# First projection block in three rounds over the banks, and two gathered blocks ahead of the first expert product

## The chip, the cores and the metric

The kernel runs on one core of one Trainium2 chip. The metric is device time in microseconds (us). TensorE is PE in the profile, VectorE is DVE, ScalarE is ACT, GpSimd is POOL, and SP is the engine whose queue issues nearly all DMAs. "PEld" is TensorE's weight load, "PEclk" its granted clock as a share of 2.4 GHz.

## What is computed

One encoder layer on 512 tokens of width 1024, all in float32. Cut to what matters here:

```python
mod = silu(c) @ w_ada + b_ada                     # shifts, scales, gates
u = x * (1.0 + sc_a) + sh_a
proj = u @ w_in                                   # queries, keys, values of two kinds of attention
mix = concat(latent_attention(proj), differential_attention(proj)) @ w_out
x = layer_norm(ALPHA * x + g_a * mix)
u = x * (1.0 + sc_f) + sh_f
aff = softmax(u @ w_router)                       # 16 experts, each takes its 64 best tokens
for e in range(16):
    xs = u[top64(aff[:, e])]
    y = (silu(xs @ w_gate[e]) * (xs @ w_up[e])) @ w_down[e]
    out[top64] += y * gate
x = layer_norm(ALPHA * x + g_f * out)
```

The expert weights (16 experts, three matrices of 8 MB each) are about 400 MB of the 456 MB that the kernel moves.

## The kernel before

**Three stages of order.** The start (the main projections, lines 425 to 483) and everything from the last output products on (router, experts, end) are written under a manual schedule: there each engine gets its instructions in the order of the text. Between them lies the attention stage. Its instructions are ordered by a scheduler that lays the program out against simulated times, so the order there depends on when it thinks the start is over.

**The start.** Inputs and weights come in 8 blocks of 128 input rows. For block i, `stage1_load` issues on SP's queue two rows of the modulation weights, the transposed input `xt` and the weights `wd`; one DMA waits for the DMA eight places ahead of it. DVE's `mod_finish` (L217) makes the block's shift and scale, and ACT (L433) makes the modulated input twice: rounded (`u.hi`) and in full (`xt`). Every float32 product is made of three products of the rounded format: both operands are split into a rounded high part and the low rest. `w_hi` on ACT (L136) and `w_lo` on DVE (L419) split the weights, L435 (DVE) makes `u.lo`. `mm3` issues the three products of one output one behind the other:

```python
    def mm3(o, l, r, start, stop):
        mm(o, l[0], r[0], start, False)
        mm(o, l[0], r[1], False, False)
        mm(o, l[1], r[0], False, stop)
```

For each block PE runs `mm3` on PSUM banks BK0 to BK3 (first half of the weights' columns), in block 0 two small products for the relative-position bias, and then `mm3` on BK4 to BK7 (second half). All products go through the helper at line 121. The banks gather over all 8 blocks and are read at the end.

In block 0, DVE's order is: shift and scale, `u.lo`, `w_lo` of the first half, `w_lo` of the second half.

**Behind the blocks.** SP's queue also carries the weights `w_q` of seven further projections (L326), and one large copy inside device memory, `bias_d<-f_d` (L481), which spreads the bias table to 512 rows of 3.5 KB. The source `f_d` is written in block 1 (L469), once DVE has copied the two small products (L145). The further projections use BK3 and BK7 in turn. Before a projection can run, ACT makes the high part of its weights (L136) and DVE the low part (L236); before its bank is used again, ACT and DVE read the bank (for keys: L136, then L501). The softmax of the differential attention is L549 (scores, PE), L564 (DVE) and L568 (ACT).

**The expert products.** 24 pages of 1 MB hold expert weights. Experts go in pairs. `up` (L1366) multiplies for each of 8 input blocks k the gathered tokens `xs[k]` with two pages (one for each expert), 16 matmuls in all, and frees both pages; SP's queue then issues the next two loads. The tokens of a pair are gathered by `gather`: 8 small matmuls for each block k with a 0/1 matrix, then one instruction of DVE (L1284, even k) or ACT (L1282, odd k) that scales and shifts. For the first pair no earlier work is there to hide the gathering, so `in_gate(k)` runs in front of product k: blocks 0 to 2 in front of product 0, then one block in front of each product, the last (block 7) in front of product 5; in front of product 7 stand the matrices for scattering back.

Of the kernel before, what the change touches and what calls it, by code (L numbers as in the profile page):

```python
# [101 lines left out]
def encoder_layer(ctx: ExitStack, tc: tile.TileContext, xT, x, wadaT, cvec, colp, rowp, rows, cst, pos, posr,  # L102
# [312 lines left out]
    def w_hi(i, c):  # L415
        EP["hi"] = hi_of(ACT, wsp[i][1].hi[:, c], st1[i][4][:, c])

    def w_lo(i, c):
        DVE.tensor_tensor(wsp[i][1].lo[:, c], st1[i][4][:, c], ff(wsp[i][1].hi[:, c]), op=OP.subtract)  # L419


    for i in range(KB):
        mw, hx, xt, hw, wd = st1[i]
        if i == 0:
            mod_finish(mw)
        if i < 2:
            w_page(i)
        if i == 0:
            w_hi(0, HALVES[0])
        uh, pg = pages.get(4, F32R)  # L430
        u = HL(pg[:, :512], pg[:, 512:])
        for dst in (u.hi, xt):
            ACT.activation(dst, xt, AF.Identity, scale=modc[:, 8 + i:9 + i], bias=modc[:, i:i + 1])  # L433
        if i < 2:
            DVE.tensor_tensor(u.lo, xt, ff(u.hi), op=OP.subtract)  # L435
            for c in HALVES:
                if i or c.start:
                    w_hi(i, c)
                w_lo(i, c)
        else:  # L440
            for c in HALVES:
                w_lo(i, c)
            DVE.tensor_tensor(u.lo, xt, ff(u.hi), op=OP.subtract)
        whh, wh = wsp.pop(i)
        U.append(u)
        Uh.append(uh)
        XT.append(xt)
        XTh.append(hx)
        pages.put(hw)
        if i + 2 < KB:  # L450
            stage1_load(i + 2)
        if 1 <= i < KB - 1:
            w_page(i + 1)
            for c in HALVES:
                w_hi(i + 1, c)
            mod_finish(st1[i + 1][0])
        for n in range(4):
            mm3(BK[n], wh[:, n * P:(n + 1) * P], u[:, :], i == 0, i == KB - 1)
        if i == 0:
            for c in range(2):  # L460
                mm(BK[6 + c][0:4, :], rb, ohp[:32, c * 512:(c + 1) * 512], True, True)
            mod_finish(st1[1][0])
            for c in range(2):
                copy(DVE, ohp[32:36, c * 512:(c + 1) * 512], BK[6 + c][0:4, :])
        for t in range(4):
            mm3(BK[4 + t], u[:, t * P:(t + 1) * P], wh[:, 512:1024], i == 0, i == KB - 1)
        pages.put(whh)
        if i == 1:
            SP.dma_start(f_d, ohp[32:36, :])  # L469
        if i == 2:  # L470
            bias_steps()
        if i == 4:
            bias_table()
        if i == 5:
            q_load(0)
            SP.dma_start(rowb[:, :R_W], bcast(rowp, R_W))
            SP.dma_start(subc, bass.AP(tensor=rowp.tensor, offset=rowp.offset + R_SUB, ap=[[1, P], [1, 1]]))
            SP.dma_start(csb, bass.AP(tensor=cst.tensor, offset=cst.offset, ap=[[C_W, P], [1, C_OH]]))
            RL = rope_load()
            q_load(1)  # L480
            SP.dma_start(bass.AP(tensor=bias_d.tensor, offset=bias_d.offset, ap=[[P * 1024, 4], [1024, P], [1, 896]]),  # L481
                         bass.AP(tensor=f_d.tensor, offset=f_d.offset + 127, ap=[[1024, 4], [-1, P], [1, 896]]))
# [1022 lines left out]
    for pr in range(NP):  # L1505
        G, U = HALF[pr % 2], HALF[1 - pr % 2]

        def in_gate(k, pr=pr, U=U):
            if pr == 0:
                gather(0, U[2:], (k + 2) * (k > 0), min(k + 3, KB))  # L1510
                if k == KB - 1:
                    scat_mats(0, *U[2:])
                return
            k0 = 3 if pr == 1 else 1
            if k0 <= k <= k0 + 3:
                for hf in range(2):
                    scatter(pr - 1, k - k0, hf, U[hf])
            elif k == k0 + 4:
                scat_mats(pr, *U[2:])
            elif k == 6 and pr == NP - 1:  # L1520
                spread(EP["l2"], U[2:], (1.0, 1.0))

        def in_up(c, G=G, U=U):
            hidden(c, U)
            if c:
                hidden_t(c - 1, G)

        def in_down(b, pr=pr, G=G):
            if b == 0:
                hidden_t(3, G)  # L1530
            if pr == NP - 1:
                if b >= 2:
                    for t in (2 * b - 4, 2 * b - 3):
                        mm(LB[t], ident, acc[t][:, 512:], True, False)
                return
            if b == 0:
                onehots(pr + 1)
            if 2 <= b <= 5:
                gather(pr + 1, G[:2], 2 * b - 4, 2 * b - 2)

        up(pr, "g", G, in_gate)
        gates(G)
        up(pr, "u", U, lambda k: None, in_up)
        down(pr, G[2:], in_down)
        if pr < NP - 1:
            for c in range(2):
                gated(c, G[2:])
        else:
            down_last()
# [78 lines left out]
```

## Time and profile before

| | |
|---|---|
| Median of 3 runs | 1246.4 us (1245.75 to 1248.85) |
| The profiled execution | 1248.78 us |
| Its span, first to last instruction | 1247.0 us |
| PE, DVE, ACT busy | 94%, 30%, 18% of the span |
| Mean granted TensorE clock | 0.989 |
| DMA | 456.03 MB, mean 366 GB/s |

Start to about 62 us, attention to about 290 us, choice of tokens to 307.6 us, experts to 1228 us, last normalisation to the end. Times in the rows are us from the span's start. In a timeline, a row begins with the start and the length of a run of equal instructions; what stands in brackets is the idle time of that engine before it and what ended it. PE's ends are modelled, so a busy PE can hide short waits.

### The profile page before, as it was taken

What the parts mean: (1) busy time and instruction counts of PE and PEld (TensorE: products, weight loads), DVE (VectorE), ACT (ScalarE), POOL (GpSimd) and SP (SyncE); (2) the same over time, 40 slices, a digit from 0 to 9 for tenths busy, and PEclk for the clock granted to TensorE, in tenths of its full rate; (3) what the DMA queues carried; (4) which work ended last, traced back from release to release, by engine and by line L of the source; (5) the groups of instructions that cost most, each with busy time, mean ns of one, the idle gap of its engine ahead of it and who ended that gap; (6) DMA issues with size and microseconds to landing.
All of it is one profiled execution on the core that took longest, in us unless ns stands there. A gap on an engine that the chain in (4) does not pass through costs nothing.

```text
span 1247.0 us, 14037 instructions
## 1 busy us (share of the span) xinstructions
PE 1166.6 (94%) x5657; PEld 553.3 (44%) x5657; DVE 373.9 (30%) x827; ACT 230.6 (18%) x473; POOL 34.0 (3%) x31
## 2 busy tenths in 40 slices
PE   8999999998999999999998899789979997999896
PEld 4877677765434333433432243234323432443232
DVE  6869989866001111111020102011101110111016
ACT  3556785433001000000000000000000000001001
POOL 0000000000000500000000000000000000000003
PEclk8999999998999999999999999999999999999999
DMA  8882516578999999999999999999999999999993
GB/s 339 307 294 74 200 62 212 195 323 342 370 420 421 420 421 421 421 421 421 420 422 420 422 421 421 422 421 421 422 421 422 421 422 420 420 422 420 422 397 144
DMA packets 76359, 456.03 MB, mean 366 GB/s; under 512 B 8284, under 2 KB 8668, under 8 KB 28162
## 3 DMA queue, kind: packets, MB, share of 16 engines
q1 hardware_dynamic: 76002, 455.02, 89.8%
q8 instruction: 44, 0.72, 0.2%
q14 instruction: 23, 0.19, 0.0%
q10 hardware_dynamic: 290, 0.10, 0.0%
HBM read 452.98 MB, written 3.95 MB: 366 GB/s over the span
## 4 chain that ended last, share of the span: by engine, by line
DMA 37%; PE 37%; DVE 1%; issue 0%; POOL 0%; ACT 0%; POOLq 0%; SPq 0%; DVEq 0%; ACTq 0%
PE bk L121 22%; DMA pg<-in_w_up_dram 18%; PE bk L1366 15%; DMA pg<-in_w_gate_dram 10%; DMA pg<-in_w_down_dram 10%; PE bk L1397 0%; DVE small L1240 0%; DVE ohg L1242 0%; POOL pg L1495 0%; DVE lst L1477 0%; PE bk L1290 0%; POOLq L1624 0%; PE bk L1315 0%; DVE mv L1478 0%; DVE pg L1434 0%
## 5 line engine op out<-in xcount | busy, mean ns | idle before, releaser
L1366 PE MATMUL bk<-pg,xs 128*64 128x512 f32 x2048 | 474.5, 601 | 50.8 <-DMA pg<-in_w_up_dram 50.7
L121 PE MATMUL bk<-pg,pg 128*64 128x512 f32 (+3 forms) x2140 | 460.7, 477 | 12.3 <-ACT pg L433 2.7
L121 PEld LDWEIGHTS bk<-pg,pg 128*64 128x64 f32 (+1 forms) x2140 | 233.6, 158 | 189.7 <-issue 133.3
L1366 PEld LDWEIGHTS bk<-pg,xs 128*64 128x64 f32 x2048 | 148.8, 137 | 348.0 <-issue 242.7
L1391 DVE TENSOR_TENSOR pg<-pg,bk 128x512 f32<-128x512 f32 x32 | 22.0, 688 | 342.3 <-PE bk L1366 314.0
L143 ACT ACTIVATE pg<-bk 128x512 f32<-128x512 f32 (+1 forms) x97 | 55.0, 581 | 356.1 <-PE bk L1397 322.3
L1284 DVE TENSOR_SCALAR xs<-bk,Gc,Bc 128x128 f32<-128x128 f32 x32 | 13.1, 409 | 207.3 <-PE bk L121 207.3
L1301 DVE TENSOR_TENSOR pg<-pg,bk 128x512 f32<-128x512 f32 x56 | 38.5, 688 | 122.4 <-PE bk L121 122.0
L121 PEld LDWEIGHTS bk<-ohg,pg 128*128 128x128 f32 x512 | 59.7, 191 | 27.3 <-issue 27.3
L121 PE MATMUL bk<-ohg,pg 128*128 128x128 f32 x512 | 66.1, 282 | 0.5 <-DVE ohg L1272 0.5
L121 PE MATMUL bk<-pg,ohg 128*128 128x512 f32 x120 | 59.2, 617 | 0.2 <-DVE pg L1434 0.2
L1282 ACT ACTIVATE xs<-bk,Bc,Gc 128x128 f32<-128x128 f32 x32 | 14.6, 457 | 200.2 <-PE bk L121 200.2
L143 ACT ACTIVATE ohg<-bk 128x512 f32<-128x512 f32 x8 | 4.8, 597 | 237.4 <-PE bk L1290 237.4
L136 ACT ACTIVATE pg<-pg 128x512 fp32r<-128x512 f32 (+2 forms) x55 | 38.3, 719 | 27.5 <-DMA pg<-in_w_q_dram 7.6
L1050 DVE CUSTOM_DVE_ANT_0 pg<-pg,pg 128x1024 f32<-128x1024 f32 x32 | 38.7, 1217 | 2.5 <-DMA pg<-in_wadaT_dram 2.5
L121 PEld LDWEIGHTS bk<-pg,ohg 128*128 128x128 f32 x120 | 20.4, 189 | 38.2 <-issue 37.6
L1434 DVE SCALAR_TENSOR_TENSOR pg<-bk,lst,pg 128x512 f32<-128x512 f32 x16 | 12.0, 751 | 74.3 <-PE bk L121 73.4
L236 DVE TENSOR_TENSOR pg<-pg,pg 128x512 fp32r<-128x512 f32 (+1 forms) x32 | 29.7, 935 | 9.3 <-ACT pg L136 9.3
L1387 ACT ACTIVATE pg<-bk 128x512 f32<-128x512 f32 x32 | 18.8, 598 | 60.1 <-PE bk L1366 60.1
L1397 PEld LDWEIGHTS bk<-csb,pg 128*128 128x128 f32 x128 | 17.7, 207 | 26.5 <-DVE pg L1391 13.5
L1451 POOL TENSOR_TENSOR pg<-pg,pg 128x512 f32<-128x512 f32 x4 | 5.1, 1275 | 786.8 <-DVE lst L1450 786.8
L568 ACT ACTIVATE pg<-pg,st 128x512 f32<-128x512 f32 x32 | 23.0, 719 | 14.4 <-DVE st L564 14.3
(224 smaller groups left out, 601.0 us busy)
## 6 DMA issues: line engine op xcount, KB each, us to landing
pg<-in_w_gate_dram SPq DMA_DIRECT2D x128, 1024.0 KB, 19.8
pg<-in_w_up_dram SPq DMA_DIRECT2D x128, 1024.0 KB, 19.8
pg<-in_w_down_dram SPq DMA_DIRECT2D x120, 1024.0 KB, 19.8
pg<-in_wadaT_dram SPq DMA_DIRECT2D x16, 1024.0 KB, 7.7
pg<-in_wadaT_dram SPq DMA_DIRECT2D x16, 512.0 KB, 8.0
pg<-in_w_down_dram SPq DMA_DIRECT2D x16, 512.0 KB, 10.8
pg<-bias_d SPq DMA_DIRECT2D x16, 256.0 KB, 3.7
pg<-in_w_out_dram SPq DMA_DIRECT2D x8, 512.0 KB, 3.3
```

The source lines that it names most:

```text
L121: PE.matmul(o, l, r, start=start, stop=stop)
L136: return ACT.activation(dst, src, AF.Copy, scale=scale)
L143: ACT.activation(dst, src, AF.Copy)
L236: lo_eng.tensor_tensor(lo, src, ff(hi), op=OP.subtract)
L568: ACT.activation(pm, pm, AF.Exp, scale=-1.0, bias=nm[:, m:m + 1], accum_out=ss[:, m:m + 1])
L1050: i = DVE.tensor_tensor_reduce(out=w2[:, j], in0=w2[:, j], in1=cs, scale=1.0, scalar=0.0, op0=OP.mult, op1=OP.add, accum_out=modr[:, n:n + 1])
L1282: ACT.activation(xs[:, k, :], src, AF.Identity, scale=Gc[:, k:k + 1], bias=Bc[:, k:k + 1])
L1301: DVE.tensor_add(acc[t][:, c], acc[t][:, c], bank)
L1366: PE.matmul(banks[c][r], xs[:, k, r], w[e][:, c * 512:(c + 1) * 512], start=k == 0, stop=k == 7)
L1387: ACT.activation(EP["HS"][:, c * 512:(c + 1) * 512], banks[c], AF.Silu)
L1391: DVE.tensor_tensor(s, s, U[c], op=OP.mult)
L1397: PE.transpose(G[c % 2][:, i * P:(i + 1) * P], sj[:, i // 2, i % 2, :], ident)
```

## The change

In block 0 of the start, the 12 matmuls on BK0 to BK3 are issued in three rounds over the four banks: high·high, then weights' low part by input's high part, then weights' high part by input's low part. The other seven blocks keep `mm3`. DVE makes the low part of the weights' first half before `u.lo` in block 0. At the first expert pair, `in_gate(0)` gathers blocks 0 and 1, and `in_gate(k)` block k + 1.

```diff
@@ block 0 of the start
         u = HL(pg[:, :512], pg[:, 512:])
+        if i == 0:
+            w_lo(0, HALVES[0])
         for dst in (u.hi, xt):
             ACT.activation(dst, xt, AF.Identity, scale=modc[:, 8 + i:9 + i], bias=modc[:, i:i + 1])
         if i < 2:
             DVE.tensor_tensor(u.lo, xt, ff(u.hi), op=OP.subtract)
-            for c in HALVES:
-                if i or c.start:
-                    w_hi(i, c)
+            for c in HALVES[i == 0:]:
+                w_hi(i, c)
                 w_lo(i, c)
...
-        for n in range(4):
-            mm3(BK[n], wh[:, n * P:(n + 1) * P], u[:, :], i == 0, i == KB - 1)
+        if i == 0:
+
+            for term in range(3):
+                for n in range(4):
+                    mm(BK[n], (wh.hi, wh.lo, wh.hi)[term][:, n * P:(n + 1) * P], (u.hi, u.hi, u.lo)[term], term == 0, False)
+        else:
+            for n in range(4):
+                mm3(BK[n], wh[:, n * P:(n + 1) * P], u[:, :], False, i == KB - 1)
@@ the first expert pair
         def in_gate(k, pr=pr, U=U):
             if pr == 0:
-                gather(0, U[2:], (k + 2) * (k > 0), min(k + 3, KB))
+                gather(0, U[2:], (k + 1) * (k > 0), min(k + 2, KB))
```

**Where instructions move: DVE in block 0.** Tile pg_11_127 is the split weights of block 0 (`w_lo`), pg_12_129 the split input (`u.lo`). Before:

```order
L226 SCALAR_TENSOR_TENSOR modc<-modr,cols 128x1
L228 TENSOR_TENSOR modc<-modr,cols 128x1
L435 TENSOR_TENSOR pg_12_129<-pg_7_111,pg_12_129 128x512
L419 TENSOR_TENSOR pg_11_127<-pg_7_111,pg_11_127 128x512 x2
L217 ISA pg_8_117,modr<-pg_8_117,pg_1_78 128x1024
```

Changed:

```order
L226 SCALAR_TENSOR_TENSOR modc<-modr,cols 128x1
L228 TENSOR_TENSOR modc<-modr,cols 128x1
L419 TENSOR_TENSOR pg_11_127<-pg_7_111,pg_11_127 128x512
L437 TENSOR_TENSOR pg_12_129<-pg_7_111,pg_12_129 128x512
L419 TENSOR_TENSOR pg_11_127<-pg_7_111,pg_11_127 128x512
L217 ISA pg_8_117,modr<-pg_8_117,pg_1_78 128x1024
```

The weights' first low part now stands ahead of the input's; nothing is added. (Line numbers of the changed kernel are up to 7 higher.)

**ACT at the beginning of the attention stage.** bk_70, bk_71 and bk_73 are BK4, BK5 and BK7, copied to free them; pg_69_2637 and pg_77_2700 are the high parts of the third and fourth of the `w_q` weights; pg_52_2479 is a table of sines; bk_69 is BK3. The first fence is before, the second the change:

```order
L143 ACTIVATE pg_65_2594<-bk_71 128x512
L136 ACTIVATE pg_69_2637<-pg_21_185 128x1024
L143 ACTIVATE pg_65_2594<-bk_73 128x512
L136 ACTIVATE pg_77_2700<-pg_7_111 128x1024
L392 ACT_TABLE_LOAD
L392 ACTIVATE pg_52_2479<-pg_52_2479 128x128
L136 ACTIVATE pg_73_2669<-bk_69 128x512
```

```order
L143 ACTIVATE pg_65_2594<-bk_71 128x512
L143 ACTIVATE pg_65_2594<-bk_73 128x512
L136 ACTIVATE pg_69_2637<-pg_21_185 128x1024
L392 ACT_TABLE_LOAD
L392 ACTIVATE pg_52_2479<-pg_52_2479 128x128
L136 ACTIVATE pg_77_2700<-pg_7_111 128x1024
L136 ACTIVATE pg_73_2669<-bk_69 128x512
```

The copy of BK7 has moved ahead of the split of the third weights, and the split of the fourth behind the sines. On DVE in the same place the low part of the third weights has moved behind four small steps of the sine table, and that of the fourth behind the table's last step; L501 still follows both.

**PE in the same place.** L549 (L556 in the changed kernel) are the six matmuls of the second scores, the rest the third of the further projections into BK3. Before:

```order
L121 MATMUL bk_69<-pg_12_129,pg_69_2637 128x512 x6
L121 MATMUL bk_69<-pg_25_220,pg_69_2637 128x512 x4
L549 MATMUL bk_68<-pg_66_2597 128x512
L549 MATMUL bk_66<-pg_66_2597 128x512
L549 MATMUL bk_68<-pg_66_2597 128x512
```

Changed:

```order
L121 MATMUL bk_69<-pg_12_129,pg_69_2637 128x512 x6
L121 MATMUL bk_69<-pg_25_220,pg_69_2637 128x512 x6
L121 MATMUL bk_69<-pg_38_306,pg_69_2637 128x512 x5
L556 MATMUL bk_68<-pg_66_2597 128x512
L556 MATMUL bk_66<-pg_66_2597 128x512
```

The second scores now follow 17 matmuls of the projection instead of 10. From here to the end of the attention stage PE, DVE and ACT have the same work in another order; SP's queue is the same up to its first six loads of bias rows. From the last output products on, the order is the text's again.

## Rows read from the trace of the kernel before

**Rows 1.** The page: GB/s moved in 40 equal slices of the span.

```profile
GB/s 339 307 294 74 200 62 212 195 323 342 370 420 421 420 421 421 421 421 421 420 422 420 422 421 421 422 421 421 422 421 422 421 422 420 420 422 420 422 397 144
```

**Rows 2.** PE's waits from 490 to 1200 us: for what, total, times, longest.

```profile
PE bk L1366 <- DMA pg<-in_w_up_dram: 50.7, 37, 2.9
```

**Rows 3.** Stretches: us, PE, PEld, DVE, ACT, POOL busy (x), PEclk, DMA share, GB/s.

```profile
20.00:44.00 24.00, 24.00 (x105) 19.26 (x104) 22.13 (x45) 11.85 (x18) 1.04 (x2) 1.00 1.03 405
62.00:290.00 228.00, 219.93 (x1397) 169.43 (x1396) 190.00 (x463) 133.85 (x306) 1.81 (x8) 0.99 0.54 195
```

**Rows 4.** Timeline of block 0 in the start, PE and DVE.

```profile
12.04 0.60 PE L121 MATMUL bk<-pg,pg 128*128 128x512 f32 x1 [2.68 <-ACT pg L433]
12.87 0.69 DVE L435 TENSOR_TENSOR pg<-pg,pg 128x512 fp32r<-128x512 f32 x1 [1.73 <-ACT pg L433]
13.48 1.28 DVE L419 TENSOR_TENSOR pg<-pg,pg 128x512 fp32r<-128x512 f32 x2
13.61 5.24 PE L121 MATMUL bk<-pg,pg 128*128 128x512 f32 x11 [0.97 <-DVE pg L435]
18.78 2.02 PE L121 MATMUL bk<-pg,rb 32*4 32x512 f32 x4
20.73 9.59 PE L121 MATMUL bk<-pg,pg 128*128 128x512 f32 x41
```

**Rows 5.** Stretches around PE's half clock in block 0, columns as rows 3.

```profile
12.00:14.00 2.00, 0.99 (x2) 0.47 (x2) 1.13 (x2) 1.33 (x2) 0.00 (x0) 0.57 0.99 390
...
18.00:20.00 2.00, 2.00 (x5) 0.38 (x5) 0.02 (x1) 1.95 (x4) 0.00 (x0) 0.72 1.04 409
```

**Rows 6.** SP's queue: two issues; a stretch, columns as rows 3; a wait.

```profile
43.26 0.79 SPq L481 DMA_DIRECT2D bias_d<-f_d  x1
44.61 8.95 SPq L326 DMA_DIRECT2D pg<-in_w_q_dram  x1
...
48.00:50.00 2.00, 2.00 (x11) 1.65 (x10) 1.64 (x2) 1.38 (x3) 0.00 (x0) 1.00 0.26 108
...
SPq L533 <- DMA bias_d<-f_d: 5.1, 1, 5.1
```

**Rows 7.** Timeline where the attention stage begins, PE, ACT and DVE.

```profile
62.65 5.73 PE L121 MATMUL bk<-pg,pg 128*128 128x512 f32 x24
67.72 1.06 ACT L136 ACTIVATE pg<-pg 128x1024 fp32r<-128x1024 f32 x1 [5.68 <-DMA pg<-in_w_q_dram]
68.81 1.23 DVE L236 TENSOR_TENSOR pg<-pg,pg 128x1024 fp32r<-128x1024 f32 x1 [6.22 <-ACT pg L136]
69.32 5.73 PE L121 MATMUL bk<-pg,pg 128*128 128x512 f32 x24 [0.93 <-ACT pg L143]
71.19 1.27 DVE L388 SCALAR_TENSOR_TENSOR pg<-pg 128x128 f32<-128x128 f32 x4
74.09 0.31 ACT L392 ACTIVATE pg<-pg 128x128 f32<-128x128 f32 x1 [0.57 <-DVE pg L391]
74.92 0.69 DVE L501 TENSOR_TENSOR pg<-bk,pg 128x512 fp32r<-128x512 f32 x1 [0.86 <-ACT pg L136]
75.67 2.58 PE L121 MATMUL bk<-pg,pg 128*128 128x512 f32 x10 [0.62 <-DVE pg L501]
```

**Rows 8.** Timeline of the first gathering and the first expert products.

```profile
307.63 2.92 PE L121 MATMUL bk<-ohg,pg 128*128 128x128 f32 x24 [0.50 <-DVE ohg L1272]
308.80 0.41 DVE L1284 TENSOR_SCALAR xs<-bk,Gc,Bc 128x128 f32<-128x128 f32 x1 [1.31 <-PE bk L121]
314.06 1.16 PE L121 MATMUL bk<-ohg,pg 128*128 128x128 f32 x8
314.16 0.80 SPq L996 DMA_DIRECT2D pg<-in_w_up_dram  x2
315.15 3.65 PE L1366 MATMUL bk<-pg,xs 128*64 128x512 f32 x16
```

**Rows 9.** The stretch with the weight stream's last pause, columns as rows 3.

```profile
314.00:316.00 2.00, 2.00 (x14) 1.31 (x14) 0.00 (x0) 0.46 (x1) 0.00 (x0) 1.00 0.46 86
```

## The prediction, made before the changed kernel ran

> **What bounds the kernel now.** Read first the data rates by slice [rows 1]: from the twelfth slice (343 us) to the last but one the core takes in 420 to 422 GB/s without a break. In that stretch the expert weights pass, and PE waits for them (50.7 us between 490 and 1200 us [rows 2]). So from about 343 us on the end is set by the moment from which the weight stream runs unbroken; PE's products after that have room. Then look for the stream's last pause: from 314 to 316 us it moved only 86 GB/s, at a DMA share of 0.46 [rows 9]. SP issues two loads at 314.16 us, just as the first expert product has ended and freed two pages (the next block's gathering starts at 314.06) [rows 8]. What comes before 314 us therefore counts in full if it moves the end of the first product, and not at all if a later wait takes it up.
>
> Two stages lie before it. In the start, PE is busy without a break from 20 to 44 us at full clock, and so is DMA (share 1.03) [rows 3]. The attention stage, 62 to 290 us, has PE busy for 219.93 of 228 us [rows 3]: 8.1 us idle.
>
> **The change part by part.** *Block 0.* PE issues one matmul at 12.04 us, then stands 0.97 us until `u.lo` is there at 13.61, and ends the twelve at 18.78 us, all but the first moments at half clock [rows 4, 5]. In rounds, the first four matmuls need only the two high parts. At full clock a matmul takes 9.59 / 41 = 0.234 us [rows 4], at half clock 0.47; four last 1.9 us, to 13.9 us. The second round needs the weights' low part: DVE stood idle 1.73 us before 12.87 us [rows 4], and one such step takes 1.28 / 2 = 0.64 us, so it fits into that idle time, as its input is the first thing ACT makes. `u.lo` is still made at 12.87 and ready at 13.56, ahead of the third round. No wait is left: twelve matmuls end at 12.04 + 5.6 = 17.7 us, 1.1 us earlier than 18.78. The clock decides how much stays. It was back at full at 18 + 2 - 2 x 0.44 = 19.1 us [rows 5], 5.5 us after the pause ended and 7.1 us after the first matmul. If it still comes at 19.1 us, the two small products now run at half clock too and the gain is some 0.5 us; if it comes 5.5 us after 12.04 us, at 17.5, another 0.8 us is won: 0.5 to 1.9 us, and I take 1.1, the value without either. On DVE and ACT nothing is added. SP's queue gains by the earlier copy into `f_d`, but its DMAs from 20 to 44 us are paced by transfers [rows 3], so its later issues stay where they are.
>
> *Where that gain goes.* At 43.26 us SP issues the copy `bias_d<-f_d`; behind it the DMA share falls to 0.26, the next issue holds the queue for 8.95 us, and the copy ends only at about 66 us [rows 6]. The third `w_q` weights stand behind it, and ACT waits 5.68 us for them, until 67.72 us [rows 7]. No instruction of PE sets these times, so they stay. In the new order the steps after 67.72 us are: ACT's high part 1.06, DVE's low part 1.23, the table's four steps 1.27, two more such steps 0.6, the sine 0.31, the high part of the fourth weights 1.06, its low part 1.23 and L501 0.69 us [rows 7], in a chain. Sum 7.45 us: PE's third projection starts at 75.2 us instead of 75.67. The copy of BK7 no longer waits behind the weights, so PE's 0.93 us pause at 69.32 goes, and its two first projections run through. They start at 62.65 - 1.1 = 61.55 and last 2 x 5.73 us, to 73.0 us. Then PE stands 2.2 us in one piece, where it stood 0.93 and 0.62. Of the 1.1 us about 0.45 us are left: I take **-0.45 us**, with ends of 0 (the chain as long as before) and -1.9 (nothing waits).
>
> *The rest of the attention stage.* The scheduler has put some hundreds of instructions in another order. The work is the same. What the order is worth no row shows; the bound on the good side is the 8.1 us of idle time [rows 3], on the bad side there is none, and the nearest row is again that idle time: it could grow as well as shrink. I take 0, and +-4, half of it, for the range. One piece can be followed: the second scores stand behind 17 matmuls of the third projection instead of 10. They begin at 75.2 + 17 x 0.24 = 79.3 us, where they began at 75.67 + 2.5 = 78.2; their softmax is later by about 1 us, and DVE has to make that up later, with 190 of 228 us busy [rows 3]. It can, but not at once.
>
> The Trainium skill, page Perfetto Trace Analysis, section Identifying the Most-Contended Engine, says that the busy share of matmuls is no good measure of PE's room, because they are pipelined, and that the weight loads' share is better. By its measure, the loads fill 19.26 / 24 = 80% of the start and 74% of the attention stage [rows 3]; at 80% the 169.43 us of loads would need 211 us, so 17 us of room and not 8.1. The sum would stay, but rival (2) below could win up to 17 us, and I would give it 0.35.
>
> *The first expert product.* A gathered block costs 315.15 - 314.06 = 1.09 us of PE [rows 8]. One of the three in front of the first product moves behind it, so this product ends 1.09 us earlier, and so do the next five; the eighth block is now gathered ahead of product 6, so products 6 and 7 end when they did. SP's two loads go out 1.09 us earlier. The stream takes 2 MB / 421 GB/s = 5.0 us for the pages of a product and PE gives up the pages of a product every 1.09 + 3.65 = 4.7 us [rows 8], so the stream stays behind PE and is not stopped again. The first product needs `xs[0]`: gathered and scaled at 308.80 + 0.41 = 309.2 us, while the second block's gathering ends at 307.63 + 16 x 0.12 = 309.5 us [rows 8]; each later block is gathered a whole product ahead. Nothing waits: **-1.09 us**, with 0 as the other end, if the stream had room at this place.
>
> **Sum.** -0.45 - 1.09 = -1.5 us on the profiled execution of 1248.78 us: 1247.3. That execution lies 2.4 us above the median of the runs, 1246.4; against the median the forecast is **1244.9 us**. Changes under 0.3%, 3.7 us, cannot be told from none here: the three runs shown spread over 3.1 us.
>
> **The rivals.** (1) *The start's gain passes on.* If the copy or the weights behind it start earlier with PE, the whole 0.5 to 1.9 us counts: 1246.4 - 1.1 - 1.1 = 1244.2, at best 1243.4. Against it stands the DMA share of 1.03 ahead of the copy [rows 3]; chance 0.12. (2) *The new order is a better one.* It closes 4 us of the 8.1 of PE's idle time: 1240.9. For it: ACT's copy of BK7 is already an example; against it: PE has little idle time by its own row. Chance 0.27, and in four of five such cases the time is under 1242.7. (3) *The longer pause halves the clock; the slow side.* Before 12.04 us PE stood 2.68 us, and its clock was halved from about 12.3 to 19.1 us [rows 4, 5]: 6.8 us that do 3.4 us of work. The pause of 2.2 us at 73 us is in one piece now. If the clock falls there, the projections behind it lose 3.4 us: 1248.3. [...] If the new order has a second such pause (the late softmax is a candidate), 3.4 us more: 1251.7. Chance 0.14, two thirds of it above 1250.1. (4) *The part at the experts does nothing.* PE's products up to 490 us are in the chain of waits as much as the stream is; if they set the end, only an order of gathering changed: 1246.0. Against it: the 420 GB/s from 343 us on [rows 1]. Chance 0.10. The forecast itself keeps 0.37.
>
> **How the numbers follow.** Faster by over 0.3%: 0.22 from (2) and 0.04 from the best ends of the forecast and of (1): 0.26. Slower: 0.10 from (3), 0.01 from the forecast's bad end: 0.11. Within: 0.63. The range leaves out the last quarter of (2) and the upper part of (3), under 2 in 10: 1240.5 to 1249.5 us; the forecast's own is 1242.5 to 1247.5.
>
> **What would show it.** In the changed kernel's profile: PE without a pause between the first matmul and the small products, block 0 some 1 us shorter; ACT's wait for `w_q` still ending near 67.7 us; PE's third projection near 75.2 us; the first expert product after 16 gathering matmuls, and SP's two loads 314.16 - 307.63 - 1.09 = 5.4 us after the first of these. If ACT's wait for `w_q` ends earlier, rival (1) holds; if PE's granted clock drops between 72 and 82 us, rival (3). The forecast is wrong if the first expert product begins more than 2 us earlier or later, against the choice of tokens, than these steps give, or if the stream pauses again after it.

## The result, and the profile after

The changed kernel takes **1258.55 us** (median of 4 runs, 1256.59 to 1259.77) against 1246.85 us before (median of 4 runs): ratio **1.0086**, 95% interval 1.0071 to 1.0102. The forecast was 1244.9 us with a range to 1249.5. The profiled execution has a span of 1256.9 us, 9.9 more than before.

First the start and the beginning of the attention stage, in the timeline of the changed kernel (PE, DVE, ACT; lines stand seven later than before). The rows answer to [rows 4, 7].

```profile
11.13 0.68 DVE L419 TENSOR_TENSOR pg<-pg,pg 128x512 fp32r<-128x512 f32 x1
12.11 5.41 PE L121 MATMUL bk<-pg,pg 128*128 128x512 f32 x12 [3.69 <-ACT pg L435]
17.45 1.87 PE L121 MATMUL bk<-pg,rb 32*4 32x512 f32 x4
...
60.28 0.97 PE L556 MATMUL bk<-pg 64*128 64x512 f32 x6
61.18 11.17 PE L121 MATMUL bk<-pg,pg 128*128 128x512 f32 x48
67.65 1.06 ACT L136 ACTIVATE pg<-pg 128x1024 fp32r<-128x1024 f32 x1 [6.59 <-DMA pg<-in_w_q_dram]
72.93 0.58 ACT L136 ACTIVATE pg<-bk 128x512 fp32r<-128x512 f32 x1
74.22 0.68 DVE L508 TENSOR_TENSOR pg<-bk,pg 128x512 fp32r<-128x512 f32 x1
74.95 5.75 PE L121 MATMUL bk<-pg,pg 128*128 128x512 f32 x17 [2.60 <-DVE pg L508]
75.92 0.69 DVE L571 CUSTOM_DVE_ANT_0 pg<-bk,pg 128x512 f32<-128x512 f32 x1 [1.02 <-DMA pg<-bias_d]
80.63 0.96 PE L556 MATMUL bk<-pg 64*128 64x512 f32 x6
```

The start did what was foretold: PE runs its twelve matmuls without a pause and is through at 17.45 instead of 18.78 us; the first scores come at 60.28 us (61.76 before). ACT's wait for the third weights ends at 67.65 us, as before, and the third projection begins at 74.95. But it runs at 0.34 us per matmul, and the second scores come at 80.63 us, 2.45 later than in the timeline of the kernel before:

```profile
78.18 0.97 PE L549 MATMUL bk<-pg 64*128 64x512 f32 x6
```

Now the whole stage, from the first scores to the first gathering matmul, in windows of the kernel before and of the changed one (columns as in rows 3).

```profile
61.76:307.63 245.87, 232.87 (x1474) 176.51 (x1474) 204.25 (x518) 142.05 (x322) 1.81 (x8) 0.98 0.57 210
```

```profile
60.28:316.56 256.28, 240.45 (x1474) 180.42 (x1474) 204.20 (x518) 142.50 (x322) 2.81 (x8) 0.97 0.56 204
```

The same 1474 matmuls take 256.28 instead of 245.87 us: **the stage is 10.4 us longer**. PE stands idle 2.8 us more (15.83 against 13.00), and it is *busy* 7.6 us more. DVE's and ACT's work is the same to half a microsecond. Where PE lost, in windows of the changed kernel (PE's busy time alone, then the granted clock, DMA share, GB/s):

```profile
72.35:74.95 2.60, 0.00 (x1) 1.00 0.54 199
75.30:78.70 3.40, 3.40 (x10) 0.50 0.89 352
...
117.00:119.70 2.70, 0.01 (x2) 1.00 0.02 6
119.80:126.40 6.60, 6.60 (x31) 0.50 0.15 47
```

Two pauses, each with half clock (1.2 GHz) behind it. Before, PE had no pause over 0.93 us at either place, no half clock at 75 us and 3.4 us of it at 118; a window of the kernel before from within that stretch:

```profile
118.20:121.40 3.20, 3.20 (x17) 0.50 0.01 2
```

A stretch at half clock does half the work (a matmul of 512 columns takes 5.24 / 11 = 0.48 us in it and 0.234 at full clock [rows 4]), so 3.4 us of it lose 1.7 us. The rest of PE's longer busy time lies at full clock, and the experiments had to find it.

The second pause, in the timeline of the changed kernel (PE, DVE):

```profile
115.92 1.22 DVE L1057 CUSTOM_DVE_ANT_0 pg<-pg,pg 128x1024 f32<-128x1024 f32 x1
...
117.67 1.22 DVE L1057 CUSTOM_DVE_ANT_0 pg<-pg,pg 128x1024 f32<-128x1024 f32 x1
...
119.02 0.68 DVE L659 TENSOR_TENSOR pg<-pg,pg 128x512 f32<-128x512 f32 x1
119.76 3.57 PE L121 MATMUL bk<-csb,pg 128*128 128x1 f32 x16 [2.74 <-DVE pg L659]
```

DVE's sum at L659, for which PE waits, stands behind two modulation reductions that nobody waits for.

Last, the experts, in the timeline of the changed kernel, which answers to [rows 8], and the lines of the kernel before that show what becomes of the gain:

```profile
316.56 2.02 PE L121 MATMUL bk<-ohg,pg 128*128 128x128 f32 x16 [0.50 <-DVE ohg L1279]
318.52 3.65 PE L1373 MATMUL bk<-pg,xs 128*64 128x512 f32 x16
322.19 10.15 SPq L1003 DMA_DIRECT2D pg<-in_w_up_dram  x6
...
350.14 0.66 PE L1297 MATMUL bk<-csb,ohg 128*128 128x128 f32 x4
...
532.25 3.60 PE L1373 MATMUL bk<-pg,xs 128*64 128x512 f32 x16
...
1244.68 5.40 PE L121 MATMUL bk<-pg,pg 128*128 128x512 f32 x8 [1.94 <-ACT pg L1493]
```

```profile
340.86 0.66 PE L1290 MATMUL bk<-csb,ohg 128*128 128x128 f32 x4
...
522.98 3.60 PE L1366 MATMUL bk<-pg,xs 128*64 128x512 f32 x16
...
1235.70 3.70 PE L121 MATMUL bk<-pg,pg 128*128 128x512 f32 x8 [1.94 <-ACT pg L1486]
```

The first gathering matmul is 8.93 us late (316.56 against 307.63), the first product 8.04 (318.52 against 310.48): 0.9 us won by gathering two blocks first. After the eighth product it is 350.14 against 340.86, **9.28 us** late: the gain is gone, and 0.35 us more. It is 9.27 us late at 523 us, and 8.98 at the last eight matmuls. These fall into half clock and take 5.40 us instead of 3.70; the span ends 9.9 us later.

### The profile page after: what moved, and what is told of

Same layout as the page of the kernel before. It is cut to its first block, busy times and chain, and to the rows that moved or that the text cites. A ratio compares the mean times of both kernels' runs of the same rounds, so it can differ in the third digit from the quotient of the medians.

```text
span 1256.9 us, 14053 instructions
## 1 busy us (share of the span) xinstructions
PE 1175.1 (93%) x5657; PEld 556.8 (44%) x5657; DVE 374.0 (30%) x827; ACT 231.1 (18%) x473; POOL 35.4 (3%) x31
## 4 chain that ended last, share of the span: by engine, by line
DMA 42%; PE 31%; DVE 1%; issue 0%; POOL 0%; ACT 0%; POOLq 0%; SPq 0%; DVEq 0%; ACTq 0%
DMA pg<-in_w_up_dram 17%; PE bk L121 17%; DMA pg<-in_w_gate_dram 13%; PE bk L1373 13%; DMA pg<-in_w_down_dram 12%; DVE small L1247 0%; DVE ohg L1249 0%; POOL pg L1502 0%; PE bk L1404 0%; DVE lst L1484 0%; PE bk L1297 0%; POOLq L1631 0%; PE bk L1322 0%; DVE mv L1485 0%; DVE pg L1441 0%
## 5 line engine op out<-in xcount | busy, mean ns | idle before, releaser
L121 PE MATMUL bk<-pg,pg 128*64 128x512 f32 (+3 forms) x2140 | 467.3, 479 | 11.1 <-ACT pg L435 3.7
L121 PEld LDWEIGHTS bk<-pg,pg 128*64 128x64 f32 (+1 forms) x2140 | 237.3, 159 | 189.8 <-issue 131.5
L121 PEld LDWEIGHTS bk<-ohg,pg 128*128 128x128 f32 x512 | 59.8, 191 | 28.1 <-issue 28.1
L121 PE MATMUL bk<-ohg,pg 128*128 128x128 f32 x512 | 66.3, 282 | 0.5 <-DVE ohg L1279 0.5
L121 PE MATMUL bk<-pg,ohg 128*128 128x512 f32 x120 | 59.2, 617 | 0.2 <-DVE pg L1441 0.2
L121 PEld LDWEIGHTS bk<-pg,ohg 128*128 128x128 f32 x120 | 20.4, 189 | 38.2 <-issue 37.5
L1394 ACT ACTIVATE pg<-bk 128x512 f32<-128x512 f32 x32 | 18.8, 598 | 60.1 <-PE bk L1373 60.1
L1404 PEld LDWEIGHTS bk<-csb,pg 128*128 128x128 f32 x128 | 17.7, 207 | 26.5 <-DVE pg L1398 13.5
```

The lines of the kernel that those rows point to most:

```text
L121: PE.matmul(o, l, r, start=start, stop=stop)
L1394: ACT.activation(EP["HS"][:, c * 512:(c + 1) * 512], banks[c], AF.Silu)
L1404: PE.transpose(G[c % 2][:, i * P:(i + 1) * P], sj[:, i // 2, i % 2, :], ident)
```

## The experiments

An order can be held. All of the stage's instructions keep their numbers in both kernels, so in most runs a table gives each engine's order, and a loop chains each instruction to the one ahead of it with an edge of issue order alone; it adds no wait. In these kernels lines stand 47 to 50 later (their L168 is L121 of the changed kernel).

```diff
+ORDER = {"PE": "2619+6 2631+3 ...", "DVE": ..., "ACT": ..., "SP": ..., "POOL": ...}
...
+    named = {i.name: i for i in nc.cur_bb.bb.instructions}
+    for runs in ORDER.values():
+        prev = None
+        for r in runs.split():
...
+                if prev is not None:
+                    tc.add_manual_dep(i, prev.name, mybir.DependencyInfo(mybir.DependencyClass.NoSync, mybir.DependencyReason.DATA))
+                prev = i
     crit = ExitStack()
```

The results, each against the kernel before on the same chip (e12 and e13 add work behind the end and are read from their traces alone):

| run | kernel | median, us | ratio, 95% interval |
|---|---|---|---|
| (changed) | the change | 1258.55 | 1.0086, 1.0071 to 1.0102 |
| e1 | the change in the old order | 1248.43 | 1.0006, 0.9992 to 1.0020 |
| e2 | before in the new order | 1258.39 | 1.0082, 1.0064 to 1.0101 |
| e3 | gather line alone | 1245.97 | 0.9988, 0.9977 to 1.0000 |
| e4 | early low part alone | 1256.74 | 1.0069, 1.0051 to 1.0087 |
| e5 | the change, third order | 1253.06 | 1.0045, 1.0030 to 1.0061 |
| e6 | the change, fourth order | 1253.94 | 1.0055, 1.0040 to 1.0070 |
| e7 | the change, DVE's sum earlier | 1256.28 | 1.0073, 1.0060 to 1.0087 |
| e8 | the change, pauses filled | 1254.27 | 1.0054, 1.0039 to 1.0069 |
| e9 | the change, evacuation ahead | 1254.76 | 1.0053, 1.0035 to 1.0070 |
| e10 | e9 and e7 together | 1254.21 | 1.0045, 1.0029 to 1.0060 |
| e11 | the change, old order mended | 1246.04 | 0.9983, 0.9972 to 0.9994 |
| e14 | before, old order mended | 1246.08 | 0.9986, 0.9975 to 0.9997 |

The stage of the main ones, from windows of each trace between its first scores and its first gathering matmul. Idle is the length less PE's busy time; lost to the clock is half of PE's busy time in the stretches at 0.50; the rest is PE's work at full clock. Changes of form count how often a matmul of PE has a weight tile of another size than the one ahead of it (128x128, 128x64, 64x128 for the most part). The expectations below count over a stretch that ends a little earlier, and so have four fewer. Each row is one execution; that of e5 was the fastest of its six (1249.66 us).

| run | stage, us | idle | lost to the clock | work at full clock | changes of form |
|---|---|---|---|---|---|
| before | 245.9 | 13.0 | 4.1 | 228.8 | 93 |
| changed | 256.3 | 15.8 | 7.2 | 233.3 | 117 |
| e1, old order | 245.7 | 14.1 | 2.4 | 229.2 | 93 |
| e2, new order | 255.9 | 15.9 | 6.4 | 233.5 | 117 |
| e5, third order | 250.5 | 19.1 | 4.4 | 227.1 | 88 |
| e6, fourth order | 255.4 | 18.8 | 10.8 | 225.8 | 88 |
| e10, new order | 253.1 | 13.5 | 6.6 | 233.0 | 117 |
| e11, old order mended | 245.8 | 13.2 | 3.9 | 228.7 | 93 |

**Order against start (e1, e2).** The theory: the new order is the loss. The rival: the earlier start is, since PE runs into the wait of 67.7 us sooner. Edits: the table above, with the old order in the changed kernel (e1) and the new one in the kernel before (e2).

> The whole change (block 0 in rounds, two gathered blocks ahead), but every engine's order in the attention stage is held to that of the kernel before by issue-order edges; nothing else differs. Theory O (the new order of the attention stage is the loss): from the first scores to the first gathering matmul the kernel before took 245.9 us and the changed one 256.3 us, so 10.4 us are the order's. Without them the time is 1258.6 - 10.4 = 1248.2, and up to 1.5 less where the start's gain passes the anchor at 67.7 us better in the old order: 1245.0 to 1248.5, the first gathering matmul 306.1 to 307.6 us. Rival S (the loss comes of the earlier start: PE runs into the 67.7 us anchor earlier, pauses 2.6 us in one piece and then works 3.4 us at half clock, whatever the order): 1250 to 1254, with the granted clock at 0.83 or so in the ten microseconds from 70 us.

> The kernel before without any part of the change, but every engine's order in the attention stage is held to that of the changed kernel. Theory O: slower by most of 10.4 us; as the start is 1.5 us later, the pause in front of the third projection is shorter by that much, so 1254 to 1258, with a pause of PE of 2.7 us near 117 to 121 us and half clock after it. Rival S (the early start is at fault): 1246 to 1249.

They settle it. The whole change in the old order cannot be told from the kernel before; the kernel before in the new order is as slow as the changed one, 0.4 us above the range expected for it. In e2's windows the stage is as long as in the changed kernel:

```profile
60.62:316.49 255.87, 239.96 (x1475) 0.97 0.56 203
```

In e1 the start's gain did not come through either. Its timeline (PE, ACT):

```profile
67.98 1.06 ACT L183 ACTIVATE pg<-pg 128x1024 fp32r<-128x1024 f32 x1 [8.27 <-DMA pg<-in_w_q_dram]
68.94 0.58 ACT L190 ACTIVATE pg<-bk 128x512 f32<-128x512 f32 x1
69.58 8.26 PE L168 MATMUL bk<-pg,pg 128*128 128x512 f32 x34 [3.52 <-ACT pg L190]
```

PE stands 3.52 us for a copy (that of bank 7) that ACT holds behind the split of weights that land at 68 us; before it was 0.93 us [rows 7]. The rival's half clock did not follow here: behind 3.52 us of pause the granted clock stayed 1.00, as a window of e1 shows (PE alone, then clock, DMA share, GB/s).

```profile
69.60:73.00 3.40, 3.40 (x15) 1.00 0.85 281
```

**Which part turned the order (e3, e4).** e3 is the kernel before with the last hunk of the change; the stage's order stays as it was. In e4 one DVE instruction of block 0 is moved, and that turns PE's order into the new one:

```diff
+        if i == 0:
+            w_lo(0, HALVES[0])
         for dst in (u.hi, xt):
...
-            for c in HALVES:
-                if i or c.start:
-                    w_hi(i, c)
+            for c in HALVES[i == 0:]:
+                w_hi(i, c)
                 w_lo(i, c)
```

> The kernel before with the gather line alone changed; the attention stage's order is that of the kernel before. If the 0.9 us that 16 instead of 24 gathering matmuls save in front of the first product pass on: 1245.9. If the weight stream takes them back (in the changed kernel the lag behind the kernel before is 8.9 us at the first gathering matmul, 8.0 at the first two experts, 9.3 at the third and 8.9 at the last): 1246.6 to 1247.2, with the last expert's products no earlier than before.

> The kernel before with only the first half's low part moved ahead of ACT's instructions in block 0; the matmuls of block 0 and the gather are as before. The scheduler gives the attention stage the same order for PE as in the changed kernel. Theory O: 1254 to 1259, as the order alone decides. Rival S: 1246 to 1248, as the start gains little without the rounds.

e4 is slower by 0.7% as expected of the order alone. e3 cannot be told from no change for certain: its interval ends at 1.0000. Its median is 1.0 us lower, but its profiled execution had no half clock at 118 us, which is worth 1.7 us and comes and goes from one execution to the next (the same stage in the same order has it in the traces of before and e13, and not in those of e3 and e12); and behind the eighth product it had lost the 0.9 us again, as the changed kernel did. e11 and e14 below speak to the same question.

**Other orders (e5, e6).** If the changes of form made the 4.5 us of work at full clock, orders with fewer of them should have it back. Edits: two more order tables in the changed kernel.

> The whole change, with the attention stage held to a third order (the one that the scheduler makes when two of the three warm-up matmuls at the start are left out; here all three are in). Changes of the weight tile's form between one matmul of PE and the next, from the first scores to the choice of experts: 84, against 89 in the kernel before and 113 in the changed one. Theory F (the 4.4 us that the new order costs at full clock are these changes of form, 24 of them at some 0.18 us each): the stage's busy time at full clock falls back to that of the kernel before or a microsecond below, and the time is 1245 to 1249 unless this order has pauses of its own. Rival (the count says nothing; only pauses and half clock do): no relation, anywhere from 1245 to 1259.

> The whole change, with the attention stage held to a fourth order (the one that the scheduler makes with six warm-up matmuls instead of three; here three are in). 84 changes of form as well, but the pieces lie elsewhere. Theory F: 1245 to 1249 again, within 2 us of the third order. Rival: anywhere from 1245 to 1259.

The work at full clock fell, to 227.1 and 225.8 us, 1.7 and 3.0 below that of before. Five fewer changes explain some 0.9 us of it at the prices measured below; what the rest is stays open. The times missed: both orders have 5 to 6 us more idle time than the old one, and the fourth loses 10.8 us to the clock. The count prices one of three parts; an order with few changes is not yet a fast one.

**The two pauses (e7, e8, e9, e10).** e7 moves DVE's sum ahead of the two reductions; e9 moves the two halves of bank 3's evacuation (ACT, DVE) ahead of the split that waits for its DMA; e10 does both. These are moves of one or two numbers in the table. e8 adds matmuls that nobody needs:

```diff
         if k1 == KB:
+            if b == 1:
+                for _ in range(10):
+                    mm(BK[5], wh.hi[:, 0:P], U[0].hi, True, True)
             pages.put(h)
...
         one = csb[:, C_ONE:C_ONE + 1]
+        for _ in range(10):
+            mm(bank, U[0].hi[:, 0:P], U[0].hi, True, True)
```

> The changed kernel in its own order, with one DVE instruction of 333 moved: the sum of the two latents' squares, which PE waited for 2.74 us at 117 us, stands ahead of two modulation reductions of 1.22 us and one softmax reduction of 0.67 us instead of behind them. If it is the order of DVE's queue that makes this pause: PE goes on at about 117 us, 2.7 us are won there, and as PE no longer stands still the half clock from 119.7 to 126.5 us shortens to 3.4 us as in the kernel before, 1.7 us more: 1254.0 to 1256.5. If the pause only moves on to the softmax that was overtaken: 1257.5 to 1259.

> The changed kernel in its own order, with ten idle matmuls of 512 columns put into each of PE's two long pauses (72.4 to 75.0 us and 117.0 to 119.8 us); their results are overwritten. They save no wait; PE only goes on working, 10 times 0.23 us each. If the pauses are what lets the clock fall: no half clock at 75.3 us (1.7 us of work won) and at most 3.4 us of it after 119 us (1.7 us won): 1254.5 to 1257.0. If the clock falls for another reason: 1258 to 1259.5.

> The changed kernel in its own order with two instructions moved: ACT's and DVE's halves of the evacuation of the first extra projection (bank 3, ready at about 67 us) stand ahead of the split of the third projection's weights, which waits for its DMA until 67.7 us, instead of behind that split and the next one. Theory: PE's pause from 72.4 to 75.0 us is bank 3 that is not yet free (its releaser is the DVE half of that evacuation), and the half clock at 75.3 us follows from the pause. Then the pause goes (2.6 us) and the half clock with it (1.7 us): 1254.0 to 1256.0, no pause of PE over 1 us between 60 and 80 us unless it is the second scores that wait for the bias until 76 us. Rival (the third weights themselves are the limit): the pause stays over 2 us and the time is 1257.5 to 1259.5.

> The same two instructions moved, and the sum of squares of run e7 as well: both long pauses of PE are attacked in the new order, with its 113 changes of form left as they are. If pauses, half clock and changes of form add up (2.8, 3.2 and 4.4 us of the 10.4): pauses and half clock go, the changes of form stay, 1250.5 to 1253.5. If the order's cost is one of pauses and clock alone: 1246 to 1248.5. If a removed pause comes back further on: 1256 to 1259.

e9 hit: 1254.76 us, some 4 us off the ratio of the changed kernel. Its timeline (PE) has 65 matmuls in one run where the pause was, and the second scores wait 1.21 us for the softmax, which waits for the bias:

```profile
60.35 15.03 PE L168 MATMUL bk<-pg,pg 128*128 128x512 f32 x65
76.59 0.96 PE L603 MATMUL bk<-pg 64*128 64x512 f32 x6 [1.21 <-DVE st L618]
```

So the third weights were not the limit. Bank 3 was, whose evacuation stood behind two splits in ACT's queue. e7 gave 1.6 us by the ratio, the low end and not clear of the noise: PE took up the sixteen matmuls at once, and then stood 1.67 us for what DVE had put off, and the half clock behind it stayed 6.8 us long (119.5 to 126.3). The timeline of e7 (PE):

```profile
116.63 1.95 PE L168 MATMUL bk<-csb,pg 128*128 128x1 f32 x16
120.24 1.11 PE L637 MATMUL bk<-csb,pg 128*128 128x128 f32 x4 [1.67 <-DVE pg L632]
```

e8's time came out as expected and 0.2 us better, but only half of its theory was tested. Its timeline (PE), and a window of it (PE alone):

```profile
74.71 5.73 PE L168 MATMUL bk<-pg,pg 128*128 128x512 f32 x17 [3.43 <-DVE pg L558]
116.67 2.57 PE L168 MATMUL bk<-pg 128*128 128x512 f32 x10
119.49 1.95 PE L168 MATMUL bk<-csb,pg 128*128 128x1 f32 x16 [0.25 <-DVE pg L709]
```

```profile
122.50:125.90 3.40, 3.40 (x18) 0.50 0.45 161
```

At 117 us the clock stayed behind the filled pause, in this one execution: the sixteen matmuls took 1.95 instead of 3.57 us, and of 6.8 us at half clock 3.4 were left. At 72 us nothing was tested: this execution's start came 3.3 us earlier, and 3.43 us of pause were left behind the ten matmuls. Nor is the 4 us by the ratio shown to be the filling's: the first gathering matmul of this execution is 1.7 us earlier than in the changed kernel's, and the other 1.9 us or so of its shorter span lie behind that, where the two kernels are the same. e10 missed its window by 0.7 us: idle time fell by 2.3 us as expected, but half clock came back, at 78.3 and at 115.9 us, so the clock's share was not won.

**The price of a change of form (e12, e13).** Groups of idle matmuls behind the last store, first with the small tiles one by one, then in pairs as the stage has them:

```diff
+            wides(48), halves(narrow, 48)
...
+            for _ in range(12):
+                wides(4), halves(narrow, 4)
```

> The kernel before with idle matmuls added behind its last store, so its time is some 60 us longer; only the added groups are read. Four groups of 48: 24 matmuls of 512 columns with a 128x128 weight tile and 24 of 128 columns with a 128x64 tile, sorted (one change of form) and alternating (47); then 24 of the former and 24 of 512 columns with a 64x128 tile, sorted and alternating. At full clock sorted groups take 24 x 0.23 + 24 x 0.06 = 7.0 us and 48 x 0.23 = 10.9 us by the stage's rows. Theory F: alternating costs 0.10 to 0.18 us more for each of the 46 further changes, 4.6 to 8.3 us more. Rival (a change of form is free, and the order's 4.4 us come from elsewhere): alternating takes as long as sorted, within 0.5 us.

> The kernel before with idle matmuls added behind its last store; only the added groups are read. Run e12 gave 0.24 us for each change to or from a 64x128 tile but 0.03 us to or from a 128x64 tile; there the small tiles stood one by one. In the attention stage they go in pairs on the two halves of the array, the 128x64 ones with unrounded f32 weights. Here both kinds stand so: 48 wide matmuls (128x128, 512 columns) and 48 half ones in pairs, sorted (one change of form), and then in 12 blocks of 4 and 4 (24 changes). Theory F (24 changes of form cost about 4.4 us in the stage): the blocks take 3.2 to 5.5 us longer than the sorted group, for either kind of half tile. Rival (128x64 tiles change freely, as in e12, and only 64x128 ones cost): the blocks with 128x64 tiles take under 1.2 us longer, those with 64x128 tiles 4 to 6 us longer, and then 2 to 3 us of the stage's 4.4 stay unexplained.

Timeline of e12 (PE): sorted and alternating with a 128x64 tile (L1510, L1512), sorted and alternating with a 64x128 tile (L1514, L1516):

```profile
1259.65 7.04 PE L1510 MATMUL bk<-pg 128*128 128x512 f32 x48
1266.52 8.34 PE L1512 MATMUL bk<-pg 128*128 128x512 f32 x48
1274.70 11.37 PE L1514 MATMUL bk<-pg 128*128 128x512 f32 x48
1286.00 22.43 PE L1516 MATMUL bk<-pg 128*128 128x512 f32 x48
```

46 further changes cost 1.3 us with the one tile and 11.1 with the other, of which some 2.2 us are the clock (0.90 over that group): 0.03 and 0.19 us each. For the tile that makes 18 of the 24 further changes this spoke against the theory. e13 has the tiles as the stage has them; its timeline (PE; an f32 matmul stands as two):

```profile
1240.95 32.98 PE L1510 MATMUL bk<-pg 128*128 128x512 f32 x144 [1.21 <-ACT pg L1504]
1273.86 5.46 PE L1514 MATMUL bk<-csb 128*64 128x128 f32 x96
...
1285.82 0.66 PE L1514 MATMUL bk<-csb 128*64 128x128 f32 x8
1286.40 1.21 PE L1510 MATMUL bk<-pg 128*128 128x512 f32 x4
...
1304.68 0.66 PE L1514 MATMUL bk<-csb 128*64 128x128 f32 x8
...
1321.81 5.76 PE L1514 MATMUL bk<-pg 64*128 64x512 f32 x48
...
1334.09 0.73 PE L1514 MATMUL bk<-pg 64*128 64x512 f32 x4
...
1353.94 0.73 PE L1514 MATMUL bk<-pg 64*128 64x512 f32 x4
```

A block of four wide and four half matmuls takes (1304.68 - 1285.82) / 11 = 1.715 us. Sorted, four wide ones take 4 x 32.98 / 144 = 0.916 and four half ones 4 x 5.46 / 48 = 0.455 us. The 0.344 us over are two changes: **0.17 us each**. With 64x128 tiles it is (1353.94 - 1334.09) / 11 - 0.916 - 4 x 5.76 / 48 = 0.408 us, **0.20 us each**. Between the orders of before and after stand 18 more changes of the first kind and 6 of the second: 18 x 0.17 + 6 x 0.20 = 4.3 us, of the 4.5 that the table shows. The traces of the stage itself bear it out. Take, for every matmul of PE, the time to the start of the next less the usual time of its like between equal tiles (idle time left out, half clock counted half). Before a matmul with another tile this excess comes to 11.5 us in all in the kernel before (93 changes), 11.6 in e1, and to 15.5 us in the changed kernel (117) and 15.6 in e2: 4.0 of the 4.5 us lie at the changes themselves. In e5 and e6 it is 11.2 and 11.0, so most of what those two orders save at full clock lies elsewhere. The Trainium skill, page TensorEngine Tiling (Array Packing), section Key Properties, says that a change of tiling mode, not of the tile alone, drains the engine. It gives no price; that e13's changes cost time agrees with it.

**A version faster than both (e11), and what the change is worth in it (e14).** e11 is e1 with three things moved in the table: ACT's copy of bank 7 and bank 3's evacuation ahead of the split, and the second scores behind 17 matmuls. e14 is the same order in the kernel before.

> The whole change with the old order of run e1, in which the evacuation of bank 3 and the last copy of the value projection stand ahead of the split that waits for its DMA, and the second scores come after 17 instead of 10 matmuls of the third extra projection. In run e1 PE paused 3.5 us at 66.1 us behind that copy. If the pause goes and the bias for the first softmax (76 us) is the next limit: second scores at 76.5 to 77.2 us instead of 77.8 with seven more matmuls done (1.6 us), 2 to 3 us won in all: 1244.0 to 1246.5, the fastest of all kernels here. If the pause only moves to the second scores: 1247 to 1249.

> The kernel before without any part of the change, with the mended old order of run e11. It tells what the change itself is worth where no order stands in its way. If the start's 1.5 us and the first expert's 0.9 us pass on once the pause at 66 us is gone: 1247.0 to 1248.5, that is 1 to 2.4 us above run e11. If the anchor at 67.7 us and the bias at 76 us still take the start's gain, and the stream the first expert's: 1245.5 to 1246.5, the same as run e11, and all of e11's gain over the kernel before is the mended order's.

Both are faster than the kernel before, by 0.17 and 0.14%, and cannot be told apart. Their profiled executions do not show where the gain lies: the first gathering comes at 305.05 and 305.06 us, in e1 at 305.12, and between 305.00 and 307.63 in the four traces of the old order with the old start (before, e3, e12, e13). PE's timeline in e11 shows no pause up to the bias:

```profile
60.17 15.03 PE L168 MATMUL bk<-pg,pg 128*128 128x512 f32 x65
76.22 0.98 PE L603 MATMUL bk<-pg 64*128 64x512 f32 x6 [1.02 <-DVE st L618]
```

The second scores come at 76.22 us with the change and at 76.18 without, though the first come at 59.27 and 60.33 us. The change itself is worth nothing that can be measured here: the two ratios differ by 0.0003, with some 0.0016 to either side, so that a gain or a loss of 1 us would not be seen.

## Why the prediction was wrong

1. *Block 0, 1.1 us with ends of 0.5 and 1.9*: right in its steps; that the size fits is in part luck. It gained 1.33 us at the twelve matmuls and 1.5 at the first scores, in one pair of executions; over all traces the first scores come at 60.18 to 62.41 us with the old start (six) and at 56.95 to 60.28 with the new one (nine).
2. *Where that gain goes*: right in its anchor and its size. ACT's wait ended at 67.65 us, the third projection began at 74.95 us (foretold 75.2), behind a pause of 2.60 us (foretold 2.2). The chain behind it was read rightly, but the chain was the order's doing and not the weights': e9 took two instructions out of it and the pause went.
3. ***The rest of the attention stage, 0 with +-4*: this step failed.** It was worth +10.4 us. The text took PE's idle time as the nearest row for what an order can change, and sized the loss by half of that. But idle time made 2.8 us of it only. The half clock made 3.1 (some 1.5 to 4.4 us are lost to it in seven traces of the old order, 6.1 to 7.7 in seven of the new), and 4.5 came as *busy* time, 4.0 of it at 24 more changes of form, a term that the sum did not have. The count needs no run: it stands in the two orders side by side, 117 against 93. Nor does a first price: in the trace of before, 93 changes exceed the usual time by 11.5 us, 0.12 us each, which makes 3 us of 24.
4. *Rival (3)* named the right mechanism for a part: the clock did fall behind the pause at 72 us, and a second pause came, though not from the late softmax but from a sum behind two reductions. Its price was too high, 3.4 us for each: that was taken from a stretch of 6.8 us. The first stretch here was 3.4 us long and cost 1.7; the second was 6.8 us long, of which the kernel before had 3.4 already.
5. *Rival (2)*, a better order, had 0.27. The rule that the prediction took from the Trainium skill, page Perfetto Trace Analysis, section Identifying the Most-Contended Engine, would have raised it to 0.35, and was no help: the room that the weight loads' share showed was not what the scheduler used. Loads were busy 180.42 us after and 176.51 before.
6. *The first expert product, -1.09 us*: the first product came 0.9 us earlier against the first gathering, SP's two loads 5.63 us after it (foretold 5.4). The text saw that products 6 and 7 end when they did, and relied on the stream to keep the gain. It did not keep it. By the eighth product PE has done the same gathering in both kernels, and one more switch between gathering and products, two changes of form, fits the 0.35 us on top (2 x 0.17). PE then waits for nothing up to 523 us in either trace, and the products that begin there are still 9.27 us late (532.25 against 522.98): up to there PE sets the time, so the step "PE's products after that have room", from 343 us on, was wrong, and rival (4) had it right. The other traces agree: counted from the first gathering, and where the clock is alike up to there, these products begin 0.3 to 0.4 us later with the new gathering than without. Only behind them does PE wait for the stream, and at the last eight matmuls the lag is 8.98 us, 0.05 more than at the first gathering. What of the 0.9 us the stream keeps in other executions, the traces do not settle.

## What to carry over

An edit ahead of an automatically ordered stage is an edit of the whole stage: here one DVE instruction moved in the start cost 0.7%. Compare the orders, count the changes of tile form on PE and price them, and hold the old order with issue-order edges to see what the edit itself is worth. A gain ahead of a fixed landing was worth nothing here until the queues behind that landing were looked through for work that was ready before it; moving two such instructions gave 4 us in the new order.

## What was not expected of the hardware

- A change between a 128x128 tile and paired half tiles costs PE 0.17 to 0.20 us at full clock (e13), and shows as busy time and not as a wait. One by one, rounded 128x64 tiles changed for 0.03 us (e12). Why these are cheaper was not tried.
- A pause does not by itself decide on the clock. With 2.60 us of pause it fell (changed kernel, 75.3 us) and with 2.37 us too (e2, 74.8 us), behind 3.52 us it stayed (e1, 69.6 us); and in the kernel before it fell at 118.1 us, though PE had not paused for longer than 0.93 us since the first scores.
- The length of half clock in block 0 differs from execution to execution (6.8 us in the kernel before, 3.4 in e12, whose start is the same), and the first scores of these kernels came anywhere between 56.95 and 62.41 us. In the new order the second scores came at 80.35 to 80.95 us all the same (changed, e2, e4, e7, e8): what the start gains is lost in front of them.
